# The state-space stage of a hybrid layer by pairs of groups: states on 128 partitions, half-array output products in fp32

## The chip, the cores and the metric

The kernel runs on one core of a Trainium2 chip. Its time is the device time of one execution in microseconds, from the first to the last instruction. A core has a matrix engine (TensorE: PE for its products, PEld for its weight loads), three elementwise engines (VectorE: DVE; ScalarE: ACT; GpSimd: POOL), a queue engine for transfers (SyncE: SP), and 16 DMA engines. Each engine works through its own instructions in a fixed order, and semaphores tie the engines together. Results of TensorE land in PSUM, all else on chip in SBUF, both with 128 partitions.

## The reference

A step of a two-layer streaming encoder: layer 0 mixes by a diagonal complex state space (S5), layer 1 by a gated delta rule. Prompt tokens (2048) and eight sample streams of 16 tokens go through together. What concerns this case is the state space of layer 0: 1024 channels in 64 groups of 16, each group with 64 complex states.

```python
def s5_branch(h, h_re, h_im, w_in, log_step, lam_re, lam_im, b_re, b_im, c_re, c_im, d, w_glu, b_glu, w_out):
    u, z = jnp.split(h @ w_in, 2, axis=-1)
    ar, ai, bbr, bbi = s5_discretize(log_step, lam_re, lam_im, b_re, b_im)
    # x_t = Abar x_{t-1} + Bbar u_t,  y_t = Re(C x_t), for every group
    y, hr, hi = s5_scan(u, h_re, h_im, ar, ai, bbr, bbi, c_re, c_im)
    y = jax.nn.gelu(y + d * u)
    y = y * jax.nn.sigmoid(y @ w_glu + b_glu)
    y = y * jax.nn.silu(z)
    return y @ w_out, hr, hi
```

## The kernel before

All of it is in fp32 in and out. The large projections are made of fp32r products: each operand is split into a high and a low part (`split_w`: ACT casts the high part, another engine subtracts for the low one), and three products, high x high, low x high, high x low, are added in PSUM (`mm3`, L146 to L148).

The program has five phases. Phase A makes u, the first half of the first projection (products `pd`), and beside it tables for the state space. Phase B is the state-space stage, and beside it the second half of that projection, the gate `z` (products `pdz`; 64 blocks of 24 products with 272 columns, `z_block`). Phase C is the gated linear unit (`pg`) and the output projection (`po`), D and E the second layer. This change touches the tables in phase A and phase B.

In phase B the tokens lie in chunks of 8; 272 columns are 256 chunks of the prompt (NPC) and 16 of the samples. A group's 16 channels by 8 positions fill 128 partitions. Phase B has 16 stages b, each for four groups, that is, two pairs pl of two groups. One stage does:

- `s5_setup`: loads the tables `sp` (powers of the transition, scaled input and output maps). From them it makes `abt` (POOL, L686 to L688), four transposes `abT` on PE (L692) into the input map `ab`, and the output map `ca` (DVE L696, POOL `cat` L697, DVE L698), which is split. The products `pk` (L704), four on a quarter of the array's columns each, give the impulse response of a chunk. It goes as `kp` to DRAM (`k_d`, issued by ACT, L711), and comes back as the Toeplitz matrix `toer` by four transfers of the SP queue (L715), which is split by ACT and POOL.
- `s5_load`: loads `u` and the rotation table `tw` (SP), and splits `u` (ACT, DVE).
- `s5_main`: four products `pb` to a pair (L744), each on half of the array's columns (weights of 64 columns), put the input of the states of two groups on 128 partitions. DVE rotates (`f` L749, `z` L750 and L751) and scans along the chunks in two segments (L767), with a carry `cy` between them (L771 to L774). `t` turns the result back (DVE L781, POOL L782). `xs` (L786 DVE, L787 POOL, on 64 partitions each) puts a group's real parts on partitions 0 to 63 and its imaginary parts on 64 to 127; then it is split. `fsp` (L788, L789) takes the last state. Last come six fp32r products to a group, three of `u` with `toe` (L798) and three of `xs` with `ca` (L800), and ACT's Gelu `y` (L801), stored by ACT's queue.

The tables are made on POOL beside phase A in eight parts (`s5_tables`, part 0 to 7), the last of them stored at L567.

A scheduler works out the order of phase B when the kernel is built, by a simulated time: stage b + 1's setup and load are issued ahead of stage b's main part, the gate blocks fill in on PE, and every engine then keeps to the order found. Pools of tiles decide when a buffer comes free: two buffers for `u`, `z`, `xs`, `toer`, `y`, one for `abt`, `kp`, and for the splits, one PSUM buffer for `pb`, two for `py`.

Of the kernel before, what the change touches and what calls it, by code (L numbers as in the profile page):

```python
# [50 lines left out]
def kernel(ctx: ExitStack, tc: tile.TileContext, I, O, upto="Z"):  # L51
    nc = tc.nc

    class Engine:
# [62 lines left out]
    d16 = cab.tile([P, 16], F32, name="d16")  # L117
    dmask = cab.tile([P, 16], F32, name="dmask")
    V.tensor_add(dmask, ident[:, 0:16], ident[:, 32:48])
    V.tensor_add(dmask, dmask, ident[:, 64:80])  # L120
    V.tensor_add(dmask, dmask, ident[:, 96:112])
# [1959 lines left out]
```

## Time and profile before

| what | value |
|---|---|
| median of three runs | 2256.23 us (2250.06 to 2259.27) |
| profiled execution, span from first to last instruction | 2257.6 us |
| its own time beside the span | the page gives none |
| PE busy in the span | 2117.6 us, 94% |
| DVE, ACT, POOL busy | 1667.1, 1001.5, 801.5 us |
| first and last gate product `pdz` start | 272.0 and 683.9 us |
| first and last rotation `f` (L749) start | 301.1 and 644.6 us |

A row of the timeline has its start, its length, the engine, the line of the kernel, the operation with output and inputs, and in brackets how long the engine sat idle before and which instruction released it. Several like instructions in a row are put together (x2, x8); a fp32 product counts as two records, a fp32r product as one. PE's lengths overlap, since products are pipelined: distances between starts are what they cost. A row of waits has the waiting engine and line, what released it, the total of the waits, how many, and the longest. PEclk is the granted TensorE clock, 1.00 at full speed.

### The profile page before, as it was taken

What the parts mean: (1) busy time and instruction counts of PE and PEld (TensorE: products, weight loads), DVE (VectorE), ACT (ScalarE), POOL (GpSimd) and SP (SyncE); (2) the same over time, 40 slices, a digit from 0 to 9 for tenths busy, and PEclk for the clock granted to TensorE, in tenths of its full rate; (3) what the DMA queues carried; (4) which work ended last, traced back from release to release, by engine and by line L of the source; (5) the groups of instructions that cost most, each with busy time, mean ns of one, the idle gap of its engine ahead of it and who ended that gap; (6) DMA issues with size and microseconds to landing.
All of it is one profiled execution on the core that took longest, in us unless ns stands there. A gap on an engine that the chain in (4) does not pass through costs nothing. (4 is left out here: it accounts for less than half of the span.)

```text
span 2257.6 us, 42148 instructions
## 1 busy us (share of the span) xinstructions
PE 2117.6 (94%) x15601; PEld 1885.4 (84%) x15601; DVE 1667.1 (74%) x3904; ACT 1001.5 (44%) x2241; POOL 801.5 (35%) x1070
## 2 busy tenths in 40 slices
PE   6999977878788999999999999999999799999998
PEld 4889966767688999999788779989987588888887
DVE  7999469999986555555764559787745778888885
ACT  3533423333335445444764432333233466666663
POOL 1267877776752322222400000100011544444430
PEclk9999998989899999999999999999999899999999
DMA  9786834344338333434265422465355644444431
GB/s 268 255 296 233 270 101 128 114 125 129 114 108 243 116 113 121 137 101 147 102 197 173 141 73 61 113 150 135 105 183 168 205 140 139 140 140 138 137 112 66
DMA packets 389402, 335.09 MB, mean 148 GB/s; under 512 B 86826, under 2 KB 350906, under 8 KB 389196
## 3 DMA queue, kind: packets, MB, share of 16 engines
q1 hardware_dynamic: 259100, 227.19, 34.1%
q10 hardware_dynamic: 127280, 96.48, 13.5%
q0 software_dynamic: 2816, 8.72, 1.2%
q8 instruction: 123, 2.02, 0.4%
q14 instruction: 83, 0.68, 0.1%
HBM read 214.57 MB, written 117.74 MB: 147 GB/s over the span
## 5 line engine op out<-in xcount | busy, mean ns | idle before, releaser
L146 PE MATMUL pc<-h1h,wdh 128*128 128x512 f32 (+1 forms) x600 | 216.2, 361 | 0.0
L148 PE MATMUL pc<-h1h,wdl 128*128 128x512 f32 (+1 forms) x600 | 215.8, 360 | 0.0
L147 PE MATMUL pc<-h1l,wdh 128*128 128x512 f32 (+1 forms) x600 | 214.9, 358 | 0.0
L1411 DVE SCALAR_TENSOR_TENSOR ac<-pb,convw,ac 128x384 f32<-128x384 f32 (+3 forms) x288 | 164.6, 595 | 3.6
L146 PE MATMUL pdz<-hhz,wzh 128*128 128x272 f32 x512 | 160.0, 313 | 2.8 <-ACT evz L643 2.8
L147 PE MATMUL pdz<-hlz,wzh 128*128 128x272 f32 x512 | 158.7, 310 | 2.8 <-DVE hlz L227 2.8
L148 PE MATMUL pdz<-hhz,wzl 128*128 128x272 f32 x512 | 158.3, 309 | 0.0
L146 PE MATMUL pg<-yh,wgh 128*128 128x272 f32 x512 | 147.8, 291 | 4.2 <-ACT evz L643 4.2
L147 PE MATMUL pg<-yl,wgh 128*128 128x272 f32 x512 | 149.1, 292 | 0.0
L148 PE MATMUL pg<-yh,wgl 128*128 128x272 f32 x512 | 148.2, 290 | 0.0
L148 PE MATMUL po<-gh,wol 128*128 128x272 f32 x512 | 147.9, 289 | 0.0
L146 PE MATMUL po<-gh,woh 128*128 128x272 f32 x512 | 147.3, 289 | 0.0
L147 PE MATMUL po<-gl,woh 128*128 128x272 f32 x512 | 147.1, 288 | 0.0
L946 POOL TENSOR_TENSOR zt<-zt,sz 128x272 f32<-128x272 f32 x64 | 59.2, 931 | 179.1 <-ACT sz L945 178.5
L146 PEld LDWEIGHTS pc<-h1h,wdh 128*128 128x128 f32 x600 | 113.1, 189 | 10.3 <-PE pc L148 0.8
L147 PEld LDWEIGHTS pc<-h1l,wdh 128*128 128x128 f32 x600 | 113.3, 189 | 10.1 <-issue 0.8
L148 PEld LDWEIGHTS pc<-h1h,wdl 128*128 128x128 f32 x600 | 113.1, 189 | 9.7
L1418 POOL COPY hout<-pb 128x3 f32<-128x3 f32 x16 | 11.6, 722 | 297.4 <-ACT pb L1401 297.4
L146 PEld LDWEIGHTS pdz<-hhz,wzh 128*128 128x128 f32 x512 | 106.7, 209 | 11.2 <-issue 7.6
L147 PEld LDWEIGHTS pdz<-hlz,wzh 128*128 128x128 f32 x512 | 106.5, 208 | 8.0 <-issue 5.0
L146 PE MATMUL pd<-hh,wuh 128*128 128x272 f32 x384 | 112.7, 294 | 0.1
L66 PE MATMUL epo<-w2h,ohi 128*128 128x512 f32 x272 | 111.5, 410 | 0.0
(635 smaller groups left out, 7040.2 us busy)
## 6 DMA issues: line engine op xcount, KB each, us to landing
wa<-in_w_ada SPq DMA_DIRECT2D x32, 512.0 KB
wdr<-in_w_in SPq DMA_DIRECT2D x24, 512.0 KB
h_d<-x ACTq DMA_DIRECT2D x8, 1088.0 KB
u_d<-ev ACTq DMA_DIRECT2D x64, 136.0 KB
hz<-h_d SPq DMA_DIRECT2D x16, 544.0 KB
u<-u_d SPq DMA_DIRECT2D x16, 544.0 KB
z_d<-evz ACTq DMA_DIRECT2D x64, 136.0 KB
y_d<-y ACTq DMA_DIRECT2D x32, 272.0 KB
```

Of the source, the lines that this page charges most:

```text
L66: i_ = f(*a, **kw)
L146: T.matmul(ps, lhsT=w_hi[k], rhs=x_hi[k], start=(k == 0), stop=False)
L147: T.matmul(ps, lhsT=w_hi[k], rhs=x_lo[k], start=False, stop=False)
L148: i_ = T.matmul(ps, lhsT=w_lo[k], rhs=x_hi[k], start=False, stop=(k == n - 1))
L946: G.tensor_mul(zt, zt, sz)
L1411: V.scalar_tensor_tensor(o, src(j), convw[:, b, j:j + 1], o, op0=ALU.mult, op1=ALU.add)
L1418: G.tensor_copy(hout[:, b, 0:3], pbt[:, 2048:2051])
```

## The change

The state-space stage is laid out by pairs of groups throughout: states stay on 128 partitions, two groups of 64, with real and imaginary parts in separate columns.

- `s5_tables` keeps powers of the transition and of the input map for pairs; the two loops over b become one, the discretisation is 32 columns wide instead of 96, and a block-diagonal copy of the input map for `pk` is added. It stays on POOL.
- `abt` and `cat` are made on DVE: four multiplications of 256 columns and one addition of 512, and four of 288 and one subtraction of 576.
- `pk` uses two column tiles, each with two products added up; `kp` has 64 partitions.
- `u`, `toe`, `ca` and `xs` are not split. A group's output is one full fp32 product of `toe` with `u` (L769 after) and two fp32 products over half of the array's rows (L773 after): group i of a pair on partitions 64 i to 64 i + 63, `tile_position=(64 * i, 0)`.
- `z` is made for both pairs at once (two operations instead of four); both `t` and both `xs` are DVE's, on 128 partitions; the two additions for the samples go from POOL to DVE, the copy of the sample states to ACT; `fsp` becomes a copy on ACT to a stage, and two DVE operations at the end.

POOL is left with two memsets in a stage. The core of the diff:

```diff
         def s5_tables(part):
...
             while n < 8:
-                for b in range(2):
-                    cmul(pv[:, 0, b, :, n + 1:2 * n + 1], pv[:, 1, b, :, n + 1:2 * n + 1],
-                         pv[:, 0, b, :, 1:n + 1], pv[:, 1, b, :, 1:n + 1],
-                         pv[:, 0, b, :, n:n + 1].broadcast_to([P, 4, n]),
-                         pv[:, 1, b, :, n:n + 1].broadcast_to([P, 4, n]),
-                         pt1[:, b, :, 0:n], pt2[:, b, :, 0:n], E=G)
+                cmul(pr[:, :, :, n + 1:2 * n + 1], pi[:, :, :, n + 1:2 * n + 1],
+                     pr[:, :, :, 1:n + 1], pi[:, :, :, 1:n + 1],
+                     pr[:, :, :, n:n + 1].broadcast_to([P, 2, 2, n]),
+                     pi[:, :, :, n:n + 1].broadcast_to([P, 2, 2, n]),
+                     pt1[:, :, :, 0:n], pt2[:, :, :, 0:n], E=G)
                 n *= 2
...
+            G.memset(sp[:, :, BDO:CCO], 0.0)
+            bv = sp[:, :, BBO:BDO].rearrange("p b (q c) -> p b q c", c=16)
+            dv = sp[:, :, BDO:CCO].rearrange("p b (q g c) -> p b q g c", g=2, c=16)
+            for g2 in range(2):
+                ln = slice(64 * g2, 64 * g2 + 64)
+                G.tensor_copy(dv[ln, :, :, g2], bv[ln])
...
         def s5_setup(b):
...
-            abt = b1.tile([P, 4, 8, 16], F32, tag="abt", name=f"abt{b}")
-            tt = b1.tile([P, 4, 8, 16], F32, tag="abtt", name=f"abtt{b}")
-            G.tensor_mul(abt, bc(gn(200, 16, 16), 2, 8), bc(gn(0, 9, 8), 3, 16))
-            G.tensor_mul(tt, bc(gn(264, 16, 16), 2, 8), bc(gn(36, 9, 8), 3, 16))
-            G.tensor_add(abt, abt, tt)
+            abt = b1.tile([P, 2, 2, 8, 16], F32, tag="abt", name=f"abt{b}")
+            tt = b1.tile([P, 2, 2, 9, 16], F32, tag="tt", name=f"abtt{b}")
+            for l in range(2):
+                V.tensor_mul(abt[:, l], bc(bc(bbv[:, 0, l], 1, 8), 1, 2), bc(pw[:, l, 0:2, 0:8], 3, 16))
+                V.tensor_mul(tt[:, l, :, 0:8], bc(bc(bbv[:, 1, l], 1, 8), 1, 2), bc(pw[:, l, 1:3, 0:8], 3, 16))
+            V.tensor_add(abt.rearrange("p l r n c -> p (l r) (n c)"), abt.rearrange("p l r n c -> p (l r) (n c)"),
+                         tt.rearrange("p l r n c -> p (l r) (n c)")[:, :, 0:128])
...
-            ca = b3.tile([P, 4, 9, 16], F32, tag="ca", bufs=2, name=f"ca{b}")
-            t2 = b1.tile([P, 4, 9, 16], F32, tag="abtt", name=f"cat{b}")
-            V.tensor_mul(ca, bc(gn(72, 16, 16), 2, 9), bc(gn(0, 9, 9), 3, 16))
-            G.tensor_mul(t2, bc(gn(136, 16, 16), 2, 9), bc(gn(36, 9, 9), 3, 16))
+            ca = b3.tile([P, 2, 2, 9, 16], F32, tag="ca", bufs=2, name=f"ca{b}")
+            t2 = b1.tile([P, 2, 2, 9, 16], F32, tag="tt", name=f"cat{b}")
+            for l in range(2):
+                V.tensor_mul(ca[:, l], bc(bc(ccv[:, 0, l], 1, 9), 1, 2), bc(pw[:, l, 1:3], 3, 16))
+                V.tensor_mul(t2[:, l], bc(bc(ccv[:, 1, l], 1, 9), 1, 2), bc(pw[:, l, 0:2], 3, 16))
             V.tensor_sub(ca, ca, t2)
-            cs_ = [b2.tile([P, 4, P], F32R, tag="ca" + i, bufs=1, name=f"ca{i}{b}") for i in "hl"]
-            split_w(*(t.rearrange("p g (n c) -> p g n c", c=16) for t in cs_), ca[:, :, 1:9])
             pk = ps_t.tile([P, P], F32, tag="t", name=f"pk{b}")
-            for g in range(4):
-                T.matmul(pk[32 * g:32 * g + 32, :], lhsT=sp[:, 200 + 16 * g:232 + 16 * g],
-                         rhs=ca[:, g, 0:8, :].rearrange("p n c -> p (n c)"), start=True, stop=True,
-                         tile_position=(0, 32 * g))
-            kp = b2.tile([P, 240], F32, tag="kp", bufs=1, name=f"kp{b}")
+            for l in range(2):
+                for r in range(2):
+                    T.matmul(pk[32 * l:32 * l + 32, :], lhsT=bdv[:, r, l],
+                             rhs=ca[:, l, r, 0:8, :].rearrange("p n c -> p (n c)"), start=(r == 0), stop=(r == 1),
+                             tile_position=(0, 32 * l))
+            kp = b2.tile([64, 240], F32, tag="kp", bufs=1, name=f"kp{b}")
             G.memset(kp[:, 0:112], 0.0)
-            S.copy(kp[:, 112:240], pk)
+            S.copy(kp[:, 112:240], pk[0:64])
...
-            toer = b2.tile([P, 4, P], F32, tag="toer", name=f"toer{b}")
-            toe = [b2.tile([P, 4, P], F32R, tag="toe" + i, bufs=1, name=f"toe{i}{b}") for i in "hl"]
+            toe = b2.tile([P, 4, P], F32, tag="toe", name=f"toe{b}")
             for g in range(4):
-                nc.sync.dma_start(toer[:, g, :], dram_ap(k_d[b], 32 * g * 240, [[16, 8], [240, 16], [1, P]]))
-            split_w(*toe, toer, G)
-            return cs_, ab, toe
+                nc.sync.dma_start(toe[:, g, :], dram_ap(k_d[b], 16 * g * 240, [[16, 8], [240, 16], [1, P]]))
+            return ca, ab, toe
         def s5_load(b):
-            ur = b2.tile([P, 4, NCH], F32, tag="ur", name=f"u{b}")
-            u = [ur] + [b2.tile([P, 4, NCH], F32R, tag="u" + i, bufs=1, name=f"u{i}{b}") for i in "hl"]
-            nc.sync.dma_start(ur.rearrange("p g c -> p (g c)"),
+            u = b2.tile([P, 4, NCH], F32, tag="ur", name=f"u{b}")
+            nc.sync.dma_start(u.rearrange("p g c -> p (g c)"),
                               dram_ap(u_d[b // 2], 4 * (b % 2) * NCH, [[8 * NCH, P], [1, 4 * NCH]]))
...
-            split_w(*u[1:], ur)
             return u, tw
...
         def s5_main(b, u, tw, ca, ab, toe):
...
+            x = b2.tile([P, 2, 2, NCH], F32, tag="x", name=f"xs{b}")
+            xh = x[:, :, :, NPC:NCH].rearrange("p l r (q h) -> p l r q h", h=2)
+            G.memset(x[:, :, :, 0:1], 0.0)
+            S.copy(xh[:, :, :, :, 0], stN[:, prs])
+            f = b2.tile([P, 2, 2, 2, NPC], F32, tag="f", name=f"f{b}")
             for pl in range(2):
                 pb_ = ps_b.tile([P, 2, 512], F32, tag="b", name=f"pb{b}_{pl}")
                 for ri in range(2):
                     for g2 in range(2):
-                        g = 2 * pl + g2
-                        T.matmul(pb_[64 * g2:64 * g2 + 64, ri, 0:NCH], lhsT=ab[:, g, 64 * ri:64 * ri + 64],
-                                 rhs=u[0][:, g], start=True, stop=True, tile_position=(0, 64 * g2))
-                S.copy(bs[:, 2 * b + pl].rearrange("p r q h -> p r (q h)"), pb_[:, :, NPC:NCH])
-                f = b2.tile([P, 2, 2, NPC], F32, tag="f", bufs=4, name=f"f{b}_{pl}")
+                        T.matmul(pb_[64 * g2:64 * g2 + 64, ri, 0:NCH], lhsT=ab[:, 2 * pl + 1 - ri, 64 * g2:64 * g2 + 64],
+                                 rhs=u[:, 2 * pl + g2], start=True, stop=True, tile_position=(0, 64 * g2))
+                bsv = bs[:, 2 * b + pl]
+                S.copy(bsv.rearrange("p r q h -> p r (q h)"), pb_[:, :, NPC:NCH])
                 for i in range(2):
-                    V.tensor_mul(seg(f[:, i]), seg(pb_[:, :, 0:NPC]), bc(bc(tw[:, pl, i], 1, 2), 1, 2))
-                V.tensor_add(z[:, pl, 0], f[:, 0, 0], f[:, 1, 1])
-                V.tensor_sub(z[:, pl, 1], f[:, 0, 1], f[:, 1, 0])
-            x = b2.tile([P, 4, NCH], F32, tag="x", name=f"xs{b}")
-            G.memset(x[:, :, 0:1], 0.0)
-            xh = x[:, :, NPC:NCH].rearrange("p g (q h) -> p g q h", h=2)
-            G.tensor_copy(xh[:, :, :, 0], stH[:, 4 * b:4 * b + 4, :])
-            xv = x.rearrange("p (l g) c -> p l g c", l=2)
-            xq = xv[:, :, :, NPC:NCH].rearrange("p l g (q h) -> p l g q h", h=2)
-            for g2 in range(2):
-                for ri in range(2):
-                    ln = slice(64 * g2, 64 * g2 + 64)
-                    G.tensor_add(xq[64 * ri:64 * ri + 64, :, g2, :, 1], ax[ln, prs, ri], bs[ln, prs, ri, :, 0])
+                    V.tensor_mul(seg(f[:, i, pl]), seg(pb_[:, :, 0:NPC]), bc(bc(tw[:, pl, i], 1, 2), 1, 2))
+                V.tensor_add(xh[:, pl, :, :, 1], ax[:, 2 * b + pl], bsv[:, :, :, 0])
+            V.tensor_add(z[:, :, 0], f[:, 0, :, 0], f[:, 1, :, 1])
+            V.tensor_sub(z[:, :, 1], f[:, 0, :, 1], f[:, 1, :, 0])
...
-            t1 = b2.tile([P, 2, 2, NPC], F32, tag="f", bufs=4, name="t1")
-            t2 = b2.tile([P, 2, 2, NPC], F32, tag="f", bufs=4, name="t2")
-            V.tensor_mul(rs(t1), rs(z), bc(tw[:, :, 0], 2, 4))
-            G.tensor_mul(rs(t2), rs(z), bc(tw[:, :, 1], 2, 4))
+            t = b2.tile([P, 2, 2, 2, NPC], F32, tag="f", name=f"t{b}")
+            for i in range(2):
+                V.tensor_mul(rs(t[:, i]), rs(z), bc(tw[:, :, i], 2, 4))
             m = NPC - 1
-            for g2 in range(2):
-                ln = slice(64 * g2, 64 * g2 + 64)
-                V.tensor_sub(xv[0:64, :, g2, 1:NPC], t1[ln, :, 0, 0:m], t2[ln, :, 1, 0:m])
-                G.tensor_add(xv[64:128, :, g2, 1:NPC], t1[ln, :, 1, 0:m], t2[ln, :, 0, 0:m])
-            V.tensor_sub(fsp[:, prs, 0], t1[:, :, 0, m], t2[:, :, 1, m])
-            V.tensor_add(fsp[:, prs, 1], t1[:, :, 1, m], t2[:, :, 0, m])
-            xs = [b2.tile([P, 4, NCH], F32R, tag="x" + i, bufs=1, name=f"xs{i}{b}") for i in "hl"]
-            split_w(*xs, x, XE(b))
-            for gp in range(2):
-                y = b2.tile([P, 2, NCH], F32, tag="y", name=f"y{b}_{gp}")
+            V.tensor_sub(x[:, :, 0, 1:NPC], t[:, 0, :, 0, 0:m], t[:, 1, :, 1, 0:m])
+            V.tensor_add(x[:, :, 1, 1:NPC], t[:, 0, :, 1, 0:m], t[:, 1, :, 0, 0:m])
+            S.copy(fe[:, :, prs], t[:, :, :, :, m])
+            for pl in range(2):
+                y = b2.tile([P, 2, NCH], F32, tag="y", name=f"y{b}_{pl}")
+                pys = [ps_y.tile([P, NCH], F32, tag="y", name=f"py{b}_{2 * pl + i}") for i in range(2)]
                 for i in range(2):
-                    g = 2 * gp + i
-                    py = ps_y.tile([P, NCH], F32, tag="y", name=f"py{b}_{g}")
-                    for wi, xi in ((0, 0), (0, 1), (1, 0)):
-                        T.matmul(py, lhsT=toe[wi][:, g], rhs=u[1 + xi][:, g], start=(wi + xi == 0), stop=False)
-                    for wi, xi in ((0, 0), (0, 1), (1, 0)):
-                        T.matmul(py, lhsT=ca[wi][:, g], rhs=xs[xi][:, g], start=False, stop=(wi == 1))
-                    S.activation(y[:, i, :], py, AF.Gelu_apprx_tanh)
+                    T.matmul(pys[i], lhsT=toe[:, 2 * pl + i], rhs=u[:, 2 * pl + i], start=True, stop=False)
+                for r in range(2):
+                    for i in range(2):
+                        ln = slice(64 * i, 64 * i + 64)
+                        T.matmul(pys[i], lhsT=ca[ln, pl, r, 1:9, :].rearrange("p n c -> p (n c)"), rhs=x[ln, pl, r],
+                                 start=False, stop=(r == 1), tile_position=(64 * i, 0))
+                for i in range(2):
+                    S.activation(y[:, i, :], pys[i], AF.Gelu_apprx_tanh)
...
+        V.tensor_sub(fsp[:, :, 0], fe[:, 0, :, 0], fe[:, 1, :, 1])
+        V.tensor_add(fsp[:, :, 1], fe[:, 0, :, 1], fe[:, 1, :, 0])
```

The order of instructions moves too. At the start of phase B on PE, before (`hhz`, `hlz` are the parts of the gate's tokens, `wzh`, `wzl` of its weights):

```order
L148 MATMUL pdz0_4_6696<-hhz0_0_6562,wzl4_4173 128x272
L692 MATMUL abT0_4266<-ident_160,abt0_4260 128x128 x4
L146 MATMUL pdz0_4_6696<-hhz0_1_6568,wzh4_4172 128x272
...
L704 MATMUL pk0_4281<-ca0_4272,sp_0_4258 32x128 x4
L744 MATMUL pb0_0_4359<-u0_4300,ab0_4265 64x272 x4
```

And after, at the same place:

```order
L149 MATMUL pdz0_2_5967<-hhz0_1_5895,wzh2_4030 128x272
L682 MATMUL abT0_4121<-ident_160,abt0_4113 128x128 x4
L150 MATMUL pdz0_2_5967<-hlz0_1_5896,wzh2_4030 128x272
...
L695 MATMUL pk0_4134<-ca0_4127,sp_0_4111 32x128 x4
L732 MATMUL pb0_0_4200<-u0_4149,ab0_4120 64x272 x4
```

The first transposes stand in the gate block 2, behind 67 gate products, where they stood in block 4, behind 108. In a later stage on PE, the outputs of the second pair of a stage, before:

```order
L798 MATMUL py6_2_5292<-uh6_5024,toeh6_5065 128x272
L798 MATMUL py6_2_5292<-ul6_5025,toeh6_5065 128x272
L798 MATMUL py6_2_5292<-uh6_5024,toel6_5066 128x272
L800 MATMUL py6_2_5292<-xsh6_5269,cah6_5050 128x272
L800 MATMUL py6_2_5292<-xsl6_5270,cah6_5050 128x272
L800 MATMUL py6_2_5292<-xsh6_5269,cal6_5051 128x272
```

And after:

```order
L732 MATMUL pb8_1_5089<-u8_4923,ab8_4936 64x272 x3
L769 MATMUL py7_2_5022<-u7_4813,toe7_4850 128x272
L773 MATMUL py7_2_5022<-xs7_4966,ca7_4833 128x272
L769 MATMUL py7_3_5023<-u7_4813,toe7_4850 128x272
L773 MATMUL py7_3_5023<-xs7_4966,ca7_4833 128x272
L773 MATMUL py7_2_5022<-xs7_4966,ca7_4833 128x272
L773 MATMUL py7_3_5023<-xs7_4966,ca7_4833 128x272
L682 MATMUL abT9_5047<-ident_160,abt9_5039 128x128 x4
L732 MATMUL pb8_1_5089<-u8_4923,ab8_4936 64x272
```

Six fp32r products to a group have become three fp32 ones, of which the half-array ones of the two groups mostly stand side by side. The stage has 281 places on PE from the first to the last `pb` where one form of product follows another (fp32r, fp32 on the full array, half columns, quarter columns, half rows); before it has 129. From phase C on, PE's order is the same.

More of the change, by code (lines that the diff above doesn't have):

```diff
@@ L82 @@
     h0_d = [dr.tile([D, NCH], F32, name=f"h0_d{i}") for i in range(8)]
-    sp_d = [dr.tile([P, 328], F32, name=f"sp_d{i}") for i in range(16)]
+    sp_d = [dr.tile([P, SPW], F32, name=f"sp_d{i}") for i in range(16)]
     tw_d = [dr.tile([P, 2, 2, SEG], F32, name=f"tw_d{i}") for i in range(16)]
@@ L91 @@
     zz_d = dr.tile([17, P, 8, P], F32, name="zz_d")
-    k_d = [dr.tile([P, 240], F32, name=f"k_d{i}") for i in range(16)]
+    k_d = [dr.tile([64, 240], F32, name=f"k_d{i}") for i in range(16)]
     nd_d = [dr.tile([4 if i < 4 else 1, 32, 1024], F32, name=f"nd_d{i}") for i in range(5)]
@@ L116 @@
     a8 = cab.tile([P, 2, 32], F32, name="a8")
[L117 to L121, printed above, removed]
+    d16 = cab.tile([64, 16], F32, name="d16")
+    dmask = cab.tile([64, 16], F32, name="dmask")
+    V.tensor_add(dmask, ident[0:64, 0:16], ident[0:64, 16:32])
+    V.tensor_add(dmask, dmask, ident[0:64, 32:48])
+    V.tensor_add(dmask, dmask, ident[0:64, 48:64])
     bglu = cst.tile([P, 8], F32, name="bglu")
@@ L527, in s5_tables @@
-            pt1 = sst.tile([P, 2, 4, 4], F32, tag="pt1", name="pt1")
-            pt2 = sst.tile([P, 2, 4, 4], F32, tag="pt2", name="pt2")
-            G.memset(pv[:, 0, :, :, 0], 1.0)
-            G.memset(pv[:, 1, :, :, 0], 0.0)
-            for h in range(2):
-                G.tensor_copy(pv[:, h, :, :, 1], abar[:, h, gs].rearrange("p (b g) -> p b g", b=2))
+            prs = slice(part * 4, part * 4 + 4)
+            sp = sst.tile([P, 2, SPW], F32, tag="sp", name=f"sp{part}")
+            pw = sp[:, :, PWO:BBO].rearrange("p b (l r n) -> p r b l n", l=2, r=3)
@@ L541, in s5_tables @@
-                n *= 2
-            ld = {}
-            for nm in ("bX1", "bX2", "cZ1", "cZ2"):
-                if nm == "cZ2":
-                    dst = sp[:, :, 136:200]
-                else:
-                    ld[nm] = dst = sst.tile([P, 2, 64], F32, tag=nm, name=f"{nm}_{part}")
-                (nc.gpsimd if part else SY).dma_start(dst, I[nm][:, gs, :].rearrange("p (b g) c -> p b (g c)", b=2))
-            x1, x2, z1 = ld["bX1"], ld["bX2"], ld["cZ1"]
-            G.tensor_scalar(sp[:, :, 72:136], z1, nsg, None, op0=ALU.mult)
@@ new lines, in s5_tables @@
+            E = nc.gpsimd if part else SY
+            bb = sst.tile([P, 2, 4, 16], F32, tag="bb", name=f"bb{part}")
+            for i in range(2):
+                E.dma_start(bb[:, i], I["bN"][:, i, prs])
+                E.dma_start(sp[:, :, CCO + 32 * i:CCO + 32 * i + 32], I["cN"][:, i, prs].rearrange("p (b l) c -> p b (l c)", b=2))
+            tb = sst.tile([P, 4, 16], F32, tag="tb", name="tb")
+            tb2 = sst.tile([P, 4, 16], F32, tag="tb2", name="tb2")
+            ov = sp[:, :, BBO:BDO].rearrange("p b (r l c) -> p r b l c", r=2, l=2)
@@ L689, in s5_setup @@
             ab = b2.tile([P, 4, P], F32, tag="ab", name=f"ab{b}")
             pt = ps_t.tile([P, 4, P], F32, tag="t", name=f"abT{b}")
-            for g in range(4):
-                T.transpose(pt[:, g, :], abt[:, g].rearrange("p n c -> p (n c)"), ident)
+            for q in range(4):
+                T.transpose(pt[:, q, :], abt[:, q // 2, q % 2].rearrange("p n c -> p (n c)"), ident)
             S.copy(ab, pt)
-            ca = b3.tile([P, 4, 9, 16], F32, tag="ca", bufs=2, name=f"ca{b}")
-            t2 = b1.tile([P, 4, 9, 16], F32, tag="abtt", name=f"cat{b}")
```

110 lines of the change are left out of this document (46 added, 64 removed).

## The prediction

> **What bounds the kernel now.** The change touches the state-space stage and the tables made for it, so I read the view by stretches of time first. Its columns are window, length, busy us of PE, PEld, DVE, ACT and POOL, granted PE clock, DMA share, GB/s.
>
> ```profile
> 260.00:280.00 20.00, 20.00 (x160) 19.01 (x160) 9.57 (x11) 8.44 (x13) 14.63 (x55) 1.00 0.96 293
> 272.00:300.00 28.00, 20.52 (x154) 19.74 (x153) 7.03 (x9) 5.38 (x11) 26.32 (x63) 0.88 0.34 116
> 300.00:684.00 384.00, 318.41 (x2218) 279.29 (x2215) 365.44 (x509) 126.29 (x265) 260.74 (x236) 0.91 0.40 122
> ```
>
> Where PE is dense (first row) 160 products take 20.0 us: 0.125 us each. From 300 to 684, 16 stages run with the gate products, and DVE is busy 365.4 of 384 us, 22.8 us a stage, while PE is not full and its clock is 0.91. What PE waited for in that stretch (total us, times, longest):
>
> ```profile
> PE py L798 <- DVE ul L127: 39.2, 13, 5.4
> PE pb L744 <- DVE f L749: 11.0, 7, 3.8
> PE pb L744 <- issue: 3.5, 2, 1.8
> PE pdz L146 <- ACT evz L643: 2.8, 2, 1.5
> PE pdz L147 <- DVE hlz L227: 2.8, 1, 2.8
> ```
>
> With five smaller rows (6.1) these are 65.4 us in some 30 waits. Next the timeline, for why DVE is full:
>
> ```profile
> 380.05 3.40 POOL L782 TENSOR_TENSOR t<-z,tw 128x1024 f32<-128x1024 f32 x1 [2.02 <-DVE z L767]
> ...
> 385.09 2.36 DVE L786 TENSOR_TENSOR xs<-t,t 64x510 f32<-64x510 f32 x2
> 385.09 3.48 POOL L787 TENSOR_TENSOR xs<-t,t 64x510 f32<-64x510 f32 x2
> 387.48 1.12 DVE L788 TENSOR_TENSOR fsp<-t,t 128x2 f32<-128x2 f32 x1
> 391.37 0.60 PE L798 MATMUL py<-ul,toeh 128*128 128x272 f32 x1 [4.67 <-DVE ul L127]
> ```
>
> An addition on two columns (L788) takes 1.12 us and ends with POOL's L787 at 388.6. The same operations alone are short, as minimum/median/maximum in ns of each line show:
>
> ```profile
> L749 DVE TENSOR_TENSOR f<-pb,tw x64: 659/678/692, 301.1 to 644.6; 128x512 f32<-128x512 f32 x64
> L767 DVE TENSOR_TENSOR_SCAN z<-rN,z x64: 392/418/1493, 306.0 to 648.2; 128x128 f32<-128x128 f32 x64
> L767 DVE TENSOR_TENSOR_SCAN z<-rN,cy,z x64: 449/460/950, 314.8 to 653.0; 128x128 f32<-128x128 f32 x64
> L781 DVE TENSOR_TENSOR t<-z,tw x16: 1219/1224/3404, 317.5 to 653.5; 128x1024 f32<-128x1024 f32 x16
> L786 DVE TENSOR_TENSOR xs<-t,t x32: 672/1674/1784, 322.6 to 661.5; 64x510 f32<-64x510 f32 x32
> L751 DVE TENSOR_TENSOR z<-f x32: 412/1068/1517, 304.6 to 646.6; 128x256 f32<-128x256 f32 x32
> L698 DVE TENSOR_TENSOR ca<-ca,cat x15: 744/750/1452, 300.5 to 626.0; 128x576 f32<-128x576 f32 x15
> L227 DVE TENSOR_TENSOR hlz<-hz,hhz x13: 1259/1279/2302, 316.4 to 650.2; 128x1088 fp32r<-128x1088 f32 x13
> ```
>
> So the stage is bound by DVE, whose work is drawn out beside POOL's, and PE loses both waits and clock.
>
> **The change: DVE.** Per stage it keeps 4 f (4 x 0.678 = 2.7) and 8 scans (4 x 0.418 + 4 x 0.460 = 3.5). z becomes two operations of f's width (1.4). t takes POOL's half over (2 x 1.224 = 2.4), x is two operations of 510 columns over all lanes (2 x 0.672 = 1.3). ca gives four multiplications of 288 columns, estimated by half of L698 and a little for the start, 0.44, and one of 0.75 (2.5); abt, from POOL, four of 256 (L751's 0.412) and one of 512 (2.3). hlz is 1.3, ten small ones 1.1. The splits of u, xs and ca go. Sum 18.5 us, 297 us in all stages, against 365 now. POOL keeps two memsets a stage, so I take the short durations; that the stretch remains is a rival. ACT loses four casts a stage and gains two small copies; it is busy a third of the time and stays hidden.
>
> **PE.** The prices, from the same timeline where PE does not wait, by starts of neighbours:
>
> ```profile
> 215.12 1.08 PE L265 MATMUL ms<-acc,onesd 128*128 128x272 f32 x4
> 216.13 1.06 PE L183 MATMUL ada<-wa,cs 128*32 128x512 f32 x8
> ...
> 400.73 0.42 PE L704 MATMUL pk<-ca,sp 128*32 128x128 f32 x8
> 401.08 0.39 PE L147 MATMUL pdz<-hlz,wzh 128*128 128x272 f32 x1
> ...
> 403.94 0.29 PE L148 MATMUL pdz<-hhz,wzl 128*128 128x272 f32 x1
> 404.06 0.60 PE L692 MATMUL abT<-ident,abt 128*128 128x128 f32 x4
> 404.42 0.37 PE L146 MATMUL pdz<-hhz,wzh 128*128 128x272 f32 x1
> 404.63 0.28 PE L147 MATMUL pdz<-hlz,wzh 128*128 128x272 f32 x1
> ...
> 405.13 0.29 PE L148 MATMUL pdz<-hhz,wzl 128*128 128x272 f32 x1
> 405.35 1.14 PE L744 MATMUL pb<-u,ab 128*64 128x272 f32 x8
> 406.41 0.39 PE L146 MATMUL pdz<-hhz,wzh 128*128 128x272 f32 x1
> 406.64 0.29 PE L147 MATMUL pdz<-hlz,wzh 128*128 128x272 f32 x1
> ```
>
> Two full fp32 products take 216.13 - 215.12 = 1.01 us, 0.505 each. Four on half the columns (pb) take 1.06, so two half-column ones run at once in 0.53. pk takes 0.35, abT 0.36. Around pb the neighbours stand 0.22 and 0.23 apart in place of 0.125: going into the tiled form costs 0.1, and leaving it 0.1. Going from fp32r into untiled fp32 (403.94 to 404.06) costs nothing, and coming back (404.42 to 404.63) 0.09. I count 0.1 for every change but the free one.
>
> First I check these prices on the kernel as it is. Gate products 1536 x 0.125 = 192; per stage 24 py products 3.0, two pb 2.12, abT 0.36, pk 0.35, in 16 stages 93; in the order of instructions 114 changes of form that cost, 11; waits 65; clock 0.09 x 384 + 0.12 x 28 = 38; and the wait for abT below, 7.5. Sum 407. These rows bound the stretch:
>
> ```profile
> 271.98 0.37 PE L146 MATMUL pdz<-hhz,wzh 128*128 128x272 f32 x1
> ...
> 274.14 1.92 DVE L696 TENSOR_TENSOR ca<-sp 128x576 f32<-128x576 f32 x2
> ...
> 284.06 1.16 POOL L567 DMA_DIRECT2D sp_d<-sp  x2 [0.21 <-POOL sp L457]
> ...
> 293.24 1.12 PE L692 MATMUL abT<-ident,abt 128*128 128x128 f32 x4 [7.49 <-POOL abt L688]
> ...
> 301.15 1.28 DVE L749 TENSOR_TENSOR f<-pb,tw 128x512 f32<-128x512 f32 x2
> ...
> 683.93 0.29 PE L147 MATMUL pdz<-hlz,wzh 128*128 128x272 f32 x1
> ```
>
> From the first gate product to the last it is 272.0 to 684.2, 412 us: the sum misses 5.
>
> Now after. Toe products: 64 x 0.505 = 32.3. The 128 half-array products are not in the trace: nothing there runs on half the rows. Counted along the order, neighbours on opposite halves pair up to 83 steps. The bounds: a step as pb's, 0.53, gives 44; no overlap at all, 128 x 0.505, gives 65. I take 44, because pb shows two independent halves of the array at work at once. pk becomes two column tiles with two serial products each, three steps: between the 0.35 of now and 3 x 0.505 x 128/272 = 0.71; I take 0.7. abT 0.36, pb 2.12. With the gate products: 192 + 34 (pb) + 32 + 44 + 6 (abT) + 11 (pk) = 319. Changes of form that cost: 236 by the order, since fp32 half-array work now stands among fp32r products, 24 us: 343 us of PE work, more than the 297 now. PE becomes the bound, DVE's 297 fits below it.
>
> Here a rule speaks against the change. The Trainium skill, "TensorEngine Tiling (Array Packing)", section "Tiling Modes", says that switching the tiling mode drains TensorE. The rows at 405 agree, with 0.1 us each way; but the 0.09 behind abT, which is untiled, the rule doesn't name. By the rule alone the 36 changes from untiled fp32 to fp32r would be free, and the sum 4 us less.
>
> For the pairs, the Trainium skill, "TensorE: Matmul & The Clock Gate", section "Part 3: Packing small matmuls", gives 3.07 times for four row tiles, not four; an estimate from it is 1.5 times for two, 0.66 a pair, with 45 pairs some 6 us more than above. No run here shows it yet.
>
> **Waits and the start.** abT0 waits 7.5 us for POOL, which is busy with tables until 285; abt is now DVE's, free from 274. In the order abT0 comes behind 67 gate products instead of 108, so at 272 + 67 x 0.125 = 280.4, when DVE has had 6 us for its 4.8 us of ca and abt. The first f then comes near 285 rather than 301, and gate products fill PE. Of the waits, those for ul, toel, xsh and xsl have lost their cause, and f's is lost with DVE's slack; evz, hlz and issue (9.1 us) may stay, and each wait has cost about 1.2 us of clock (38 over 30), so 15 us if all stay and 0 if none does. I take 9. Gate products then end at 272 + 343 + 9 = 624 instead of 684.2: 60 us earlier. What follows has the same order on PE and shifts whole; the part before 272 is PE-dense and keeps its products. 2257.6 - 60 = 2197.6 against the profiled span (nothing lies around it on the page); the median is 1.4 below it: **2196 us**. All waits or none: 2187 to 2203; with changes at 0.05 and 0.15 each, 2175 to 2214.
>
> **Rivals.** *Half-array products run one after the other.* 65 instead of 44: 2217. For it: they share the columns and write two banks, and only column halves are seen to overlap. Against it: pb.
>
> *DVE stays drawn out* because its own operands and not POOL make it so. Then z, x, kp, cy and the scans keep about 5 us a stage of stretch: 23.5 us a stage, no less than the 22.8 of now; only the start is gained, 301 - 285 = 16: 2241. Against it: every long L788 or L786 ends with a POOL row.
>
> *The Toeplitz blocks come late*, the other side. toe goes through DRAM: SP waits for the store of kp before it can load, and the queue holds the loads of u, tw and sp behind it.
>
> ```profile
> SPq L715 <- DMA k_d<-kp: 74.1, 16, 13.5
> ```
>
> The mean wait is 4.6 us, the longest 13.5. In the new order the first toe product of an even stage stands only some 35 products behind its pk, and PE works in order, so gate products queue behind it. Were each of eight such waits 13.5 - 4.6 = 8.9 us longer than what covers it, with 1.2 of clock, it would cost 81: 2196 + 81 = 2277. It decides from 60/8 - 1.2 = 6.3 us a time. Against it: pk no longer waits for a full DVE, and toer's casts are gone from the path.
>
> **How the numbers follow.** Forecast 0.58, serial halves 0.20, drawn-out DVE 0.13, Toeplitz 0.09. The forecast's own range is 2175 to 2214; with serial halves (2217) and their waits it reaches 2230. 0.5% (11 us) is what can be told from no change: below 2245 counts as faster. Faster: 0.58 + 0.20 + two thirds of 0.13 = 0.86; same: the rest of it and a mild Toeplitz wait, 0.07; slower 0.07.
>
> **What would show it.** DVE below 300 us busy in the stage, no small DVE operation drawn out beside a POOL row, first f near 285; PE clock 0.97 or more; last gate product near 624. Serial halves: two half-array products 1.0 us apart instead of 0.53. Toeplitz: a wait of PE at the toe products, released by DMA. I am wrong if PE idles more than 25 us in the stage, or if a change of form costs other than 0.1.

## The result and the profile after

The changed kernel takes 2194.72 us in the median of four runs (2190.02 to 2196.93), the kernel before, on the same chips, 2253.82 (2250.06 to 2259.27): a ratio of 0.9734, with a 95% interval of 0.9715 to 0.9754. Forecast were 2196 us, with 2175 to 2214 as the forecast's own range and up to 2230 with serial halves.

The whole gain lies where it was looked for. The first product of phase C (`pg`) starts at 623.1 instead of 688.55 us, 65.5 earlier, and the span is 2192.2 instead of 2257.6, 65.4 shorter; from `pg` to the end both take 1569.1. That match is by luck: in the thirteen profiled executions of this document the part from `pg` on takes 1559 to 1581 us, though its code is the same in all. The profiled execution of the kernel before was also the slowest of its four, so the medians lie 59.1 us apart, not 65. The view by stretches of time of the changed kernel (columns as in the prediction), and all waits of PE from 272 to 640 (total, times, longest):

```profile
272.00:300.00 28.00, 27.96 (x222) 24.70 (x220) 25.00 (x56) 6.77 (x18) 5.37 (x10) 1.00 0.58 183
300.00:624.00 324.00, 320.21 (x2161) 249.64 (x2160) 251.89 (x532) 90.18 (x231) 12.28 (x35) 1.00 0.47 143
```

```profile
PE py L773 <- DVE xs L762: 2.5, 1, 2.5
PE pg L149 <- ACT evz L630: 1.3, 1, 1.3
```

DVE is 78% busy (251.9 of 324 us), where it was 95%. PE is full and its clock is 1.00, where it was 0.91. Of some 77 us of waits (65.4 in the stages, 7.5 for abT0, 4.2 ahead of `pg`) 3.8 are left, and none is a wait for a Toeplitz block. DVE's lines, as minimum, median and maximum in ns:

```profile
L737 DVE TENSOR_TENSOR f<-pb,tw x64: 679/683/694, 286.8 to 595.1; 128x512 f32<-128x512 f32 x64
L760 DVE TENSOR_TENSOR t<-z,tw x32: 1216/1219/1227, 299.1 to 608.5; 128x1024 f32<-128x1024 f32 x32
L762 DVE TENSOR_TENSOR xs<-t x16: 677/682/691, 302.5 to 609.8; 128x510 f32<-128x510 f32 x16
L750 DVE TENSOR_TENSOR cy<-z,tw x16: 144/161/516, 296.0 to 602.8; 128x4 f32<-128x4 f32 x16
```

The medians now stand at the minima: `xs`, which took 1674 ns in the median on 64 lanes, takes 682 on 128, and the first `f` starts at 286.8 instead of 301.1. The products on PE, in a stretch without a wait:

```profile
430.18 0.29 PE L151 MATMUL pdz<-hhz,wzl 128*128 128x272 f32 x1
430.31 0.62 PE L769 MATMUL py<-u,toe 128*128 128x272 f32 x2
430.86 0.72 PE L773 MATMUL py<-xs,ca 64*128 64x272 f32 x2
431.51 0.73 PE L769 MATMUL py<-u,toe 128*128 128x272 f32 x2
432.17 1.18 PE L773 MATMUL py<-xs,ca 64*128 64x272 f32 x6
433.28 0.39 PE L149 MATMUL pdz<-hhz,wzh 128*128 128x272 f32 x1
...
439.70 0.28 PE L149 MATMUL pdz<-hhz,wzh 128*128 128x272 f32 x1
439.91 0.73 PE L773 MATMUL py<-xs,ca 64*128 64x272 f32 x4
440.57 0.39 PE L150 MATMUL pdz<-hlz,wzh 128*128 128x272 f32 x1
440.89 0.73 PE L773 MATMUL py<-xs,ca 64*128 64x272 f32 x4
```

Two records are one fp32 product. A single half-array product (430.86) keeps PE for 0.65 us, two of them on opposite halves (439.91) for 0.66: they run at once. Three, in two steps (432.17), take 1.11, so a step (one product, or two on opposite halves) is some 0.455. The price beside it is that of coming and going: from 439.91 to 440.89 there is one pair and one fp32r product, 0.98 - 0.125 = 0.855, so a visit (one or more steps in a row, from leaving the fp32r products to being back at them) costs 0.4 beyond its steps. The prediction had two changes for it, 0.2.

### The profile page after: what moved, and what is told of

It reads as the page before. It is cut to its first block, busy times and chain, and to the rows that moved or that the text cites. A ratio compares the mean times of both kernels' runs of the same rounds, so it can differ in the third digit from the quotient of the medians.

```text
span 2192.2 us, 41754 instructions
## 1 busy us (share of the span) xinstructions
PE 2119.9 (97%) x15601; PEld 1855.7 (85%) x15601; DVE 1548.0 (71%) x3968; ACT 961.9 (44%) x2209; POOL 508.5 (23%) x738
## 5 line engine op out<-in xcount | busy, mean ns | idle before, releaser
L149 PE MATMUL pdz<-hhz,wzh 128*128 128x272 f32 x512 | 151.7, 298 | 0.0
L150 PE MATMUL pdz<-hlz,wzh 128*128 128x272 f32 x512 | 151.5, 297 | 0.0
L151 PE MATMUL pdz<-hhz,wzl 128*128 128x272 f32 x512 | 151.1, 296 | 0.0
L150 PE MATMUL pd<-hl,wuh 128*128 128x272 f32 x384 | 110.8, 289 | 0.3 <-DVE hl L230 0.3
L151 PE MATMUL pd<-hh,wul 128*128 128x272 f32 x384 | 110.9, 289 | 0.0
L1386 DVE TENSOR_SCALAR ac<-pb,convw 128x512 f32<-128x512 f32 (+2 forms) x96 | 39.1, 421 | 101.2 <-ACT pb L1378 60.3
L69 PE MATMUL epo<-w2h,olo 128*128 128x512 f32 x272 | 106.9, 393 | 0.0
```

The source lines that it names most:

```text
L69: i_ = f(*a, **kw)
L149: T.matmul(ps, lhsT=w_hi[k], rhs=x_hi[k], start=(k == 0), stop=False)
L150: T.matmul(ps, lhsT=w_hi[k], rhs=x_lo[k], start=False, stop=False)
L151: i_ = T.matmul(ps, lhsT=w_lo[k], rhs=x_hi[k], start=False, stop=(k == n - 1))
L1386: V.tensor_scalar(o, src(0), convw[:, b, 0:1], None, op0=ALU.mult)
```

## Experiments

Each comparison is with the kernel before on the same chip. Where no time of the changed kernel is named, it is the 2194.72 above (ratio 0.9734).

### The two parts of the change one by one

**Without splits, on the kernel before.** The old layout has a group's real and imaginary parts on 128 partitions, so an unsplit output needs only two products on the whole array.

```diff
...
-                    for wi, xi in ((0, 0), (0, 1), (1, 0)):
-                        T.matmul(py, lhsT=toe[wi][:, g], rhs=u[1 + xi][:, g], start=(wi + xi == 0), stop=False)
-                    for wi, xi in ((0, 0), (0, 1), (1, 0)):
-                        T.matmul(py, lhsT=ca[wi][:, g], rhs=xs[xi][:, g], start=False, stop=(wi == 1))
+                    T.matmul(py, lhsT=toe[:, g], rhs=u[:, g], start=True, stop=False)
+                    T.matmul(py, lhsT=ca[:, g, 1:9, :].rearrange("p n c -> p (n c)"), rhs=x[:, g],
+                             start=False, stop=True)
```

> One part alone on the kernel before: u, toe, ca and xs unsplit, and each group's output two fp32 products over the whole array (toe with u, ca with xs; the old layout has a group's real and imaginary parts on 128 partitions) in place of six fp32r ones. POOL keeps its half of t and xs. My theory (DVE binds): DVE loses ul, cal and xsl, 3.8 us a stage, 22.8 to 19.0, 304 us; PE work 192 + 32 x 1.26 (pb) + 16 x 0.55 (pk) + 16 x 0.45 (abT) + 128 x 0.455 + some 75 changes x 0.09 = 313, so both are near each other and the stage ends near 610: 2180 to 2195. Rival (what paid is taking POOL's work over, not the splits): DVE stays drawn out and full, no more than 15 us gained: 2240 or more, and 2270 if PE's 15 us more of work shows.

Measured: 2205.35 us, ratio 0.9798 (0.977 to 0.9825). 45 us come from dropping the splits alone, with t and xs still on POOL, so the rival that the gain is in taking these over is out. (One split, toel, was POOL's own: 16 operations of 1.49 us in the median, so POOL's load fell a little too.) But it is 10 us slower than my bound. What is left is a wait of PE for POOL's half of xs, and its view by stretches shows DVE no longer full and a clock of 0.96:

```profile
PE py L790 <- POOL xs L781: 18.0, 13, 3.8
...
300.00:600.00 300.00, 273.96 (x1815) 223.08 (x1814) 251.18 (x433) 71.32 (x179) 203.31 (x206) 0.96 0.45 140
```

**t and xs on DVE, on the kernel before**, splits kept:

```diff
-            G.tensor_mul(rs(t2), rs(z), bc(tw[:, :, 1], 2, 4))
+            V.tensor_mul(rs(t2), rs(z), bc(tw[:, :, 1], 2, 4))
...
-                G.tensor_add(xv[64:128, :, g2, 1:NPC], t1[ln, :, 1, 0:m], t2[ln, :, 0, 0:m])
+                V.tensor_add(xv[64:128, :, g2, 1:NPC], t1[ln, :, 1, 0:m], t2[ln, :, 0, 0:m])
```

> The other part alone: the kernel before with t and xs all on DVE, splits and six fp32r products kept. My theory (DVE is drawn out beside POOL): its work at short durations is 20.2 us a stage, with 1 to 2.5 of stretch beside abt, cat and toel, against 22.8 now: 2215 to 2255, faster by 0 to 40. Rival (its length is its own): 24.1 + 1.2 + 1.4 = 26.7 us a stage, 2315.

Measured: 2232.87 us, ratio 0.9919 (0.9899 to 0.9939), 18 us faster although DVE was the bound and got 1.22 + 2 x 0.67 = 2.6 us more a stage to do. Its lines:

```profile
L786 DVE TENSOR_TENSOR xs<-t,t x32: 669/685/1460, 313.7 to 637.5; 64x510 f32<-64x510 f32 x32
...
L788 DVE TENSOR_TENSOR fsp<-t,t x16: 161/163/165, 317.3 to 638.9; 128x2 f32<-128x2 f32 x16
...
L771 DVE TENSOR_TENSOR cy<-z,tw x16: 161/1004/1078, 306.1 to 628.8; 128x4 f32<-128x4 f32 x16
```

The same xs took 1674 ns in the median and the same fsp 1117 while POOL ran t and its half of xs; now they take 685 and 163. cy keeps its 1004: in that order it stands beside POOL's abt, as before (432.60 to 433.67 in one stage, POOL's L688 432.36 to 433.65). DVE's length was POOL's doing.

**Both at once, on the kernel before.**

> The same with t and xs all on DVE; abt and cat stay on POOL. My theory: DVE's work at its short durations is some 17 us a stage with 1 to 2 of stretch beside POOL's four remaining operations, 295; PE 313 binds: stage end near 600, 2170 to 2180, below the changed kernel's 2195, whose half-array products cost more PE time (347) than full ones. Rival (DVE's length is its own, not POOL's): DVE gets 16 x 2.6 us more than in the run without it and ends near 345: 2215 or more.

Measured: 2179.2 us, ratio 0.9687 (0.9665 to 0.971), within what was expected, and below the changed kernel: the intervals do not touch. Together the parts give 71.5 us, more than 45 + 18: with both, the waits for xs are short (5.4 us for DVE's xs) and PE is at 289 of 300 us with a clock of 1.00.

```profile
300.00:600.00 300.00, 289.09 (x2014) 241.68 (x2012) 281.64 (x505) 81.12 (x196) 110.85 (x171) 1.00 0.50 153
```

### POOL beside DVE

One of the two t multiplications of the changed kernel goes back to POOL:

```diff
-            for i in range(2):
-                V.tensor_mul(rs(t[:, i]), rs(z), bc(tw[:, :, i], 2, 4))
+            for i, e in ((0, V), (1, G)):
+                e.tensor_mul(rs(t[:, i]), rs(z), bc(tw[:, :, i], 2, 4))
```

> The changed kernel with one of its two t multiplications back on POOL. My theory (DVE operations are drawn out while a POOL operation on SBUF runs): POOL's row of 3.4 us is there again once a stage, DVE's t or the operations beside it that now take 0.68 (z, xs) or 0.16 (small ones) read 1 us and more at the median or the upper end, while the line with no POOL operation beside it keeps 0.68; DVE loses 1.22 a stage and gets back 1 to 2, and has a wait for POOL in its chain. PE binds and hides most of it: 2190 to 2215. Rival (the drawn-out rows of before come from DVE's own operands): no line on DVE gets longer than it is in the changed kernel, and the time is 2190 to 2197.

Measured: 2197.91 us, ratio 0.9767 (0.9752 to 0.9781). The rival falls, but my expectation was too broad: z and xs keep their medians, since in this order they seldom stand beside POOL. What stands there is drawn out (its timeline, DVE and POOL):

```profile
351.28 1.23 DVE L760 TENSOR_TENSOR t<-z,tw 128x1024 f32<-128x1024 f32 x1
352.42 3.47 DVE L230 TENSOR_TENSOR hlz<-hz,hhz 128x1088 fp32r<-128x1088 f32 x1
...
351.38 3.37 POOL L760 TENSOR_TENSOR t<-z,tw 128x1024 f32<-128x1024 f32 x1 [9.39 <-ACT hhz L230]
...
298.81 1.23 DVE L760 TENSOR_TENSOR t<-z,tw 128x1024 f32<-128x1024 f32 x1
299.95 1.28 DVE L737 TENSOR_TENSOR f<-pb,tw 128x512 f32<-128x512 f32 x2
...
298.91 3.38 POOL L760 TENSOR_TENSOR t<-z,tw 128x1024 f32<-128x1024 f32 x1 [3.02 <-DMA toe<-k_d]
```

hlz, 1.29 us in the median, takes 3.47 and ends 1.14 us after POOL's row (355.89 and 354.75), not far from its own length. DVE's t, which began 0.10 before POOL's, keeps 1.23. And f, which reads one operand from PSUM, keeps 0.64 each beside the same POOL row. The Trainium skill, "SBUF — State Buffer", section "Who interferes with whom", says that a VectorE instruction with two SBUF inputs contends with a GpSimd instruction that reads SBUF, and that one with at most one, outside VectorE's two-port modes, does not. Of these modes it says that whoever issues first holds the shared pair for the whole instruction while the other waits. These rows agree with the first two points, and hlz shows a wait for a whole instruction. But the wait doesn't always go by who began first: in another stage of the same run POOL's t began before DVE's t and ca, which kept their lengths, and took 5.15 us itself.

```profile
506.69 5.15 POOL L760 TENSOR_TENSOR t<-z,tw 128x1024 f32<-128x1024 f32 x1 [11.07 <-issue]
507.65 1.22 DVE L760 TENSOR_TENSOR t<-z,tw 128x1024 f32<-128x1024 f32 x1
508.79 0.82 DVE L688 TENSOR_TENSOR ca<-sp 128x288 f32<-128x288 f32 x2
```

### Whether PE is the bound now

**DVE's t made twice**, so that DVE does 39 us more:

```diff
-            for i in range(2):
+            for i in (0, 1, 0, 1):
                 V.tensor_mul(rs(t[:, i]), rs(z), bc(tw[:, :, i], 2, 4))
```

> The changed kernel with DVE's two t multiplications made twice, 16 x 2.44 = 39 us more of DVE and nothing else. My theory (PE binds now, DVE is 78% busy): DVE work 280 + 39 = 319 stays below PE's 347: 2190 to 2207, the upper end if the chain of the last stage shows. Rival (DVE still sets the pace of the stage): 39 us more, 2225 to 2240.

Measured: 2208.4 us, ratio 0.979 (0.9766 to 0.9814): 14 us slower than the changed kernel, a third of the work added, and 1 us above my upper end. PE is full from 300 to 600; what the stage loses, it loses at its end, where PE waits for xs of the last stage. The first `pg` starts at 628.6, only 5.6 us later than in the changed kernel; the rest of the 14 us lies behind the stage, where nothing was changed, and its cause stays open.

```profile
300.00:600.00 300.00, 300.00 (x2079) 238.61 (x2079) 267.78 (x539) 82.59 (x216) 4.02 (x28) 1.00 0.47 143
...
PE py L773 <- DVE xs L762: 7.7, 1, 7.7
```

**Without the toe products.**

```diff
-                for i in range(2):
-                    T.matmul(pys[i], lhsT=toe[:, 2 * pl + i], rhs=u[:, 2 * pl + i], start=True, stop=False)
...
-                                 start=False, stop=(r == 1), tile_position=(64 * i, 0))
+                                 start=(r == 0), stop=(r == 1), tile_position=(64 * i, 0))
```

> The changed kernel without the 64 products of toe with u, so the outputs lack the part of the input of the same chunk; kp, its way through DRAM and all of DVE's work stay. My theory (PE binds): 64 x 0.455 + some 37 x 0.09 = 32 us of PE work less, 315 left, with DVE at 280 to 290: 25 to 32 us faster, 2163 to 2172. Rival (DVE or the transfers set the pace, PE only looks full): 0 to 8 us faster, 2187 to 2195.

Measured: 2156.97 us, ratio 0.9566 (0.9541 to 0.9591): 37.7 us less than the changed kernel, 6 more than I had and below the range. PE is the bound. A count made afterwards gives the 6 us a price in the order: without toe, 117 visits of tiled products become 100 and 25 changes from fp32 to fp32r are gone, 17 x 0.4 + 25 x 0.09 = 9, and 64 x 0.455 + 9 = 38.

### Whether half-array products overlap

Two versions of the changed kernel hold the four half-array products of a pair in an order, first alternating between the halves, then two on the same half (`T.ordered` makes PE keep the written order):

```diff
-                for r in range(2):
-                    for i in range(2):
-                        ln = slice(64 * i, 64 * i + 64)
+                T.ordered, T.last = True, None
+                for r, i in ((0, 0), (0, 1), (1, 0), (1, 1)):
+                    ln = slice(64 * i, 64 * i + 64)
...
+                T.ordered = False
```

> The control for the next run: the changed kernel with the four half-array products of a pair held in the order (upper, lower, upper, lower half of the rows). Neighbours on opposite halves pair up to 80 steps where the changed kernel has 83, in 59 visits where it has 60. Both theories: as the changed kernel, 2190 to 2198.

The second has `((0, 0), (1, 0), (0, 1), (1, 1))` there.

> The same products held in the order (upper, upper, lower, lower): 111 steps instead of 80 in 65 visits instead of 59; the rest of PE's work is the same. My theory (products on opposite halves of the rows run at once, a step is 0.455, PE binds): 31 x 0.455 + 6 x 0.4 = 16 us above the control, 2207 to 2213; in the trace a visit with one product per half takes 0.66, one with two on the same half 1.1. Rival (they run one after the other anyway): 2 us above the control, 2192 to 2200.

Measured: 2192.92 us (ratio 0.9723, 0.9701 to 0.9745) and 2209.76 us (0.9797, 0.9775 to 0.982), 16.8 us apart, where 16 were expected of products that overlap and 2 of products that don't. In the stage itself, from the first gate product to the first `pg`, the profiled executions are 11.9 us apart (350.8 and 362.7), which still leaves the rival out. In the trace of the second, a visit of two products on the same half lasts 1.11 us, from its start to the next row, against 0.66 for one on each half:

```profile
435.32 1.18 PE L69 MATMUL py<-xs,ca 64*128 64x272 f32 x4
436.43 0.39 PE L151 MATMUL pdz<-hhz,wzl 128*128 128x272 f32 x1
```

### Full products in place of half-array ones

In the changed kernel x is written in the old layout (four DVE operations on 64 lanes) and ca copied so by ACT:

```diff
...
-            V.tensor_sub(x[:, :, 0, 1:NPC], t[:, 0, :, 0, 0:m], t[:, 1, :, 1, 0:m])
-            V.tensor_add(x[:, :, 1, 1:NPC], t[:, 0, :, 1, 0:m], t[:, 1, :, 0, 0:m])
+            for g2 in range(2):
+                ln = slice(64 * g2, 64 * g2 + 64)
+                V.tensor_sub(x[0:64, :, g2, 1:NPC], t[ln, 0, :, 0, 0:m], t[ln, 1, :, 1, 0:m])
+                V.tensor_add(x[64:128, :, g2, 1:NPC], t[ln, 0, :, 1, 0:m], t[ln, 1, :, 0, 0:m])
...
-                for r in range(2):
-                    for i in range(2):
-                        ln = slice(64 * i, 64 * i + 64)
-                        T.matmul(pys[i], lhsT=ca[ln, pl, r, 1:9, :].rearrange("p n c -> p (n c)"), rhs=x[ln, pl, r],
-                                 start=False, stop=(r == 1), tile_position=(64 * i, 0))
+                for i in range(2):
+                    T.matmul(pys[i], lhsT=ca[:, pl, i].rearrange("p n c -> p (n c)"), rhs=x[:, pl, i],
+                             start=False, stop=True)
```

> The changed kernel with outputs by full products: x is written in the old layout, a group's real parts on partitions 0 to 63 and imaginary on 64 to 127 (four DVE operations on 64 lanes in place of two on 128), ca is copied so by ACT, and each group has one fp32 product of ca with x over the whole array in place of two over half the rows. My theory (PE binds, and the half-array products cost 83 steps x 0.455 + 60 visits x 0.4 = 62 us): in place of it 64 x 0.455 + 40 x 0.09 = 33 us, so PE work falls from 347 to 317, with DVE near 305: 2195 - 27 = 2168, no less than 2160. Rival (half-array pairs are as cheap as a full product, and something else sets the end): 2190 to 2200, or slower by DVE's 1.4 us a stage, 2215.

Measured: 2189.43 us, ratio 0.9721 (0.9685 to 0.9757), not to be told from the changed kernel: a miss. PE did get time back: the last gate product starts at 583.6, where it was 621.5, 38 us earlier. Some 7 us of that are products of the last stage that now stand behind it, and 2 are waits, so PE's work fell by some 29, where 30 were expected (347 to 317). But the last stage was not done then (timeline and waits of PE):

```profile
583.60 0.28 PE L151 MATMUL pdz<-hhz,wzl 128*128 128x272 f32 x1
588.61 2.08 PE L738 MATMUL pb<-u,ab 128*64 128x272 f32 x8 [4.72 <-DVE f L743]
...
607.56 2.60 PE L782 MATMUL py<-xs,cf 128*128 128x272 f32 x4 [10.15 <-DVE xs L774]
...
612.63 0.49 PE L149 MATMUL pg<-yh,wgh 128*128 128x272 f32 x1
```

The gate products had run out, and PE stood beside DVE's chain of the last stage. The first `pg` comes 10 us earlier than in the changed kernel (612.6 and 623.1), and the phases behind it took 12 us more in this execution (1581.0 and 1569.1). To see whether the end of the stage is where the gain went, the last 4 or 6 gate blocks were issued behind the last `pb`:

```diff
...
         while zst["n"] < 64:
-            z_block()
+            with later([zst["pb"]] if zst["n"] >= 64 - 4 else []):
+                z_block()
```

> The same with 4 blocks held, 12 us of PE. My theory: 6 to 10 us earlier than without, 2179 to 2184. Rival: 2186 to 2195.

> The kernel with full products, with the last 6 of the 64 gate blocks (6 x 3 us on PE) issued only behind the last input product pb of the last stage. There the gate blocks had run out at 583.6, and PE stood idle for some 20 us beside DVE's chain of the last stage. My theory (the gain of the full products was lost there): PE fills that stretch, the end of the stage comes 8 to 15 us earlier: 2174 to 2182. Rival (DVE's total sets the end, wherever PE's gate blocks stand): PE idles as long ahead of the last stage, 2186 to 2195.

Measured: with 4 held 2178.4 us, ratio 0.9679 (0.9664 to 0.9693); with 6 held 2188.98 us, 0.9734 (0.9714 to 0.9754). Four blocks bring about 0.4% against none (0.9721; the intervals overlap). PE's wait for DVE's xs falls from 10.5 to 1.3 us, but 9.2 us of waits for u and f appear ahead of the last two groups of `pb`, and the first `pg` starts at 609.9, only 2.7 us earlier than without; so it isn't shown that holding blocks back pays. Six bring nothing: PE stands idle ahead of the last `pb` instead, for u of the last two stages and for f, as the rival said. That part of the gain is lost at the end of the stage is shown by the 10 us wait above; filler held back moves the gap:

```profile
562.16 2.08 PE L738 MATMUL pb<-u,ab 128*64 128x272 f32 x8 [4.83 <-DMA u<-u_d]
572.87 2.05 PE L738 MATMUL pb<-u,ab 128*64 128x272 f32 x8 [2.21 <-DMA u<-u_d]
578.97 2.08 PE L738 MATMUL pb<-u,ab 128*64 128x272 f32 x8 [4.05 <-DVE f L743]
```

Of the runs that compute the whole result, the full products with 4 blocks held and the kernel before with unsplit products and DVE's t and xs are the fastest, both with intervals wholly below that of the changed kernel, and not to be told from each other.

## Why the prediction was right

**The bound.** That DVE bound the stage, drawn out by POOL, stands: taking t and xs from POOL made DVE's other lines short at once, and the time fell though DVE had more to do. One reading was loose: of the drawn-out rows only those of L788 end with a POOL row, while the long ones of L786 end mostly 0.55 us behind one, as if their work began when POOL's was done. That PE binds after the change stands too: 39 us more of DVE cost 14, and without the toe products, 38 us of PE, the kernel is 37.7 faster.

**DVE's sum.** 18.5 us a stage in durations was forecast, 297 us in all; the profile has 25.0 + 251.9 = 277 us busy between 272 and 624. Busy time counts overlapping ends once; added up by durations, DVE's rows there are 316 us, of which 13 are splits for the projections, so the like figure is 303, near the 297.

**PE's sum** was 343 us of work; the profile gives 350.9 from the first gate product (272.2) to the first `pg` (623.1), less 3.8 of waits: 347. The sum came out near by errors that cancel, which is luck. *The full product* was taken as 0.505, from a pair of `ms` with a tiled product behind it; it is 0.455 (in the run with full products, neighbours start 0.46 apart, at 595.12 and 595.58). *The step* of half-array products was taken as 0.53, from pb with part of its own changes in it; it is 0.455. Together 64 x 0.05 + 83 x 0.075 + 64 x 0.075 (pb) = 14 us too much. *pk* was taken as three steps, 0.7; it keeps PE for 0.57, two steps of some 0.214 (0.455 by the width) and a part of its changes, 4 us too much in steps. *The change of form* was taken as 0.1; a visit of a half-array product between fp32r products costs 0.4, one of pb 1.51 - 0.25 - 2 x 0.455 = 0.35 (from the prediction's rows at 405). With 60 visits of half-array products and 57 of pb and pk, 24 + 20 us, and 38 changes from fp32 to fp32r at 0.09, 3, the changes come to 47 us instead of 24. "A change of form costs other than 0.1" was one of the prediction's own signs of being wrong, and in this term it was. By these prices the work is 192 (gate) + 29 (pb, 64 steps) + 29 (toe) + 38 (83 steps) + 6 (abT) + 7 (pk, two steps) + 47 = 348, 1 above the 347 measured; they are read from the same trace, so this closes the sum and doesn't test it. The same prices give 31 x 0.455 + 6 x 0.4 = 16.5 us for the products apart (16.8 measured), and 38 for the run without toe (37.7).

**The waits.** Of the 9.1 us that could stay (evz, hlz, issue) none did; 3.8 others came. I had taken 9 for waits and clock. The clock is 1.00; 0.97 or more was forecast.

**The time.** In the profiled pair the stage became 65.5 us shorter, where 60 were forecast; the check of the prices on the kernel before had missed 5 as well. The medians lie 59.1 apart. That 2196 meets 2194.72 to a microsecond is luck within this spread.

**Where the time came from.** PE's work rose from 192 + 32 x 1.26 + 16 x (0.55 + 0.45 + 3.0) = 296 to 347, 51 more; the waits fell from 77 to 4; and the 38 us of lost clock came back. 51 - 73 - 38 = -60, of 65.5 measured.

**The rivals.** Serial half-array products are out by the two orders. DVE drawn out by its own operands is out by the kernel before with t and xs on DVE. Late Toeplitz blocks did not show: SP's wait for kp's store is a little shorter, and none of PE's waits is for a toe block; their weight loads waited for one once, 0.5 us.

```profile
SPq L705 <- DMA k_d<-kp: 64.1, 16, 9.3
```

**What was not foreseen** is that the half-array part of the change is no gain: the same layout of x as before, with unsplit products on the whole array, needs less of PE, some 29 us.

## What to carry to other kernels

Look at what an elementwise engine's rows end with: where VectorE's small operations end together with GpSimd's, taking GpSimd's work over can shorten VectorE's own time. When the bound moves to TensorE, count how often the form of its products changes: a half-array product saved nothing here against a full one, since each visit cost 0.4 us beyond its 0.455 us step. And once an engine has room, look at the end of the stage, where the filler work may run out before the last chain is done.

## What the runs showed of the hardware

Two fp32 products on opposite halves of the rows take the time of one (0.66 against 0.65 us from start to next start), and two on the same half 1.11. The Trainium skill, "TensorE: Matmul & The Clock Gate", section "Part 3: Packing small matmuls", gives 3.07 times for four row tiles; two here overlap wholly, and what is lost is lost in going to the tiled form and back, 0.4 us a visit between fp32r products. The prediction's estimate from that figure, 0.66 a pair, is met only by chance, since a lone product keeps PE as long. Not every VectorE operation is held up by a GpSimd one: f, with one operand in PSUM, kept 0.64 us beside it, while hlz, with both in SBUF, went from 1.29 to 3.47. And it is not always VectorE that waits: GpSimd's t, 3.38 us in most stages of that run, took 5.15 in one where VectorE's operations ran on beside it.
